# Half of the modulation's weight pieces multiplied in plain f32, and the small first loads issued by ScalarE

## The chip, the cores and the metric

The kernel runs on one core of a Trainium2 chip. The metric is the device time of one execution in microseconds, the lower the better. The engines are named as the profile does: PE is TensorE (PEld its loading of weights), DVE is VectorE, ACT is ScalarE, POOL is GpSimd and SP is SyncE, which issues nearly all DMA transfers here.

## The reference, cut to what matters

The kernel computes one layer of a generator block over 1024 latent tokens and 256 context tokens, each of width 1024. Everything begins with the modulation: a conditioning vector `c` for the latent tokens and `c_ctx` for the context go through SiLU and are multiplied by the same weight `w_ada` of 1024 x 6144.

```
mod  = silu(c)     @ w_ada + b_ada
modc = silu(c_ctx) @ w_ada + b_ada
sh1, sc1, gt1, sh2, sc2, gt2 = split(mod, 6)          # csh1, csc1, ... = split(modc, 6)
h  = rmsnorm(x,   g_mix) * (1 + sc1)  + sh1
hc = rmsnorm(ctx, g_mix) * (1 + csc1) + csh1
p  = h @ w_in                                         # and columns of hc @ w_in
...                                                   # three groups of heads, w_out, residual, mixture of experts
```

The change lies in the first third of `mod` and `modc`: the columns 0 to 2047 of `w_ada`, which give `sh1` and `sc1` for both kinds of token. Nothing of the projection `h @ w_in` can begin before they are there.

## The kernel before, in words

The kernel goes through the modulation and the norm of the tokens (lines 245 to 347), the four projections by 512 columns of `w_in` (lines 349 to 510), the three head groups, and the experts. In the part that is touched the order of the instructions on each engine comes from the tile framework, which orders them by a timeline of its own; the head groups and the experts have an order written by a planner in the kernel and are not touched.

**The modulation.** The 2048 columns are four groups `g` of 512, and each group has eight pieces `k` of 128 rows: 32 pieces of 128x512 f32, 256 KB each. SP loads them (line 239), the first five ahead of everything else (line 250). A piece goes into one of 21 slices of buffers that are needed only later (`bu`, `qc`, `yc`, `vc`, `kc`); the pieces 21 to 31 use the slices of the pieces 0 to 10 a second time.

PE multiplies in a reduced form of f32 (`fp32r`) in the kernel before. To keep the precision a piece is split in two: ACT copies it into `wh`, rounded (line 227), and DVE subtracts, which gives the rest `wl` (line 228). For some pieces of `w_in` POOL does the subtraction.

```
def split_piece(w, slow=False):
    h = wspl.tile([128, 512], F32R, name="wh")
    l = wspl.tile([128, 512], F32R, name="wl")
    nc.scalar.activation(h, w, AF.Copy)
    (nc.gpsimd if slow else nc.vector).tensor_sub(l, w, f32(h))
    return h, l
```

The stationary operand is `csx`, four columns for each `k`: the rounded SiLU of `c` and of `c_ctx`, and the rests of both. Two products for each piece add into `pm`, 4x512 in PSUM (line 299): `csx` with `wh` for all four rows, and the two rounded columns with `wl` for the first two rows.

`csx` comes from six small transfers into `rows`, a tile of 48x128 (lines 252 to 257): `c`, `c_ctx`, a part of `b_ada`, `g_mix`, and `bs_tok` twice. PE transposes `rows` (line 259), DVE copies it to `cols` (261), ACT applies SiLU, which needs a load of its table (263), and DVE makes `csx` (266, 267).

After the eight pieces of a group DVE copies `pm` to `mr` (306), PE transposes it in four steps into `acc` (308), and DVE adds the bias and makes the shift `mcol` and the scale `acol` (311 to 316). The tile `mr` and the tile `hf` below have one common buffer (tag `hf`, one buffer).

**The tokens.** Tiles of 128 tokens are loaded (`load_x`, line 272), the two context tiles first, among the pieces of the last group; ACT and DVE make the norm, PE transposes (330), ACT applies scale and shift into `hf` (334), and DVE splits it as well (345, 346). The first projection product (line 377) needs this for the first half of the first context tile, and the split pieces of `w_in`, whose loads stand on SP behind the pieces of the modulation.

Of the kernel before, what the change touches and what calls it, by code (L numbers as in the profile page):

```python
# [11 lines left out]
F32 = mybir.dt.float32  # L12
# [11 lines left out]
KD = D // 128  # L24
# [130 lines left out]
def f32(ap):  # L155
    return ap.bitcast(F32)
# [7 lines left out]
def block_kernel(ctx: ExitStack, tc: tile.TileContext, A, out):  # L164
    nc = tc.nc
# [47 lines left out]
    with ExitStack() as p1:  # L213
# [10 lines left out]
# [6 lines that stand above are left out]
# [7 lines left out]
        def load_piece(c0, k, src="w_in"):  # L237
            w = early.pop(0) if early else wraw.tile([128, 512], F32, name="wr")
            nc.sync.dma_start(w, A[src][0, k * 128:(k + 1) * 128, c0:c0 + 512])
            return w  # L240
# [4 lines left out]
        with ExitStack() as p0:  # L245
            stage = p0.enter_context(tc.tile_pool(name="stage", bufs=2))
# [2 lines left out]

            ahead = [load_piece(0, k, "w_ada") for k in range(AH)]  # L250
            rows = stage.tile([48, 128], F32, bufs=1)
            nc.sync.dma_start(rows[0:8], A["c"].rearrange("a (k p) -> (a k) p", p=128))
            nc.sync.dma_start(rows[8:16], A["c_ctx"].rearrange("(k p) -> k p", p=128))
            nc.sync.dma_start(rows[16:32], A["b_ada"][0:1, 0:2048].rearrange("a (k p) -> (a k) p", p=128))
            nc.sync.dma_start(rows[32:40], A["g_mix"].rearrange("a (k p) -> (a k) p", p=128))
            nc.sync.dma_start(rows[40:44], A["bs_tok"][0])
            nc.sync.dma_start(rows[44:48], A["bs_tok"][0])
            pr = psT.tile([128, 512], F32, name="pT")
            nc.tensor.transpose(pr[:, :48], rows, ident[:48, :48])
            cols = consts.tile([128, 48], F32)  # L260
# [3 lines left out]
            cs2 = cs.rearrange("p (j k) -> p k j", j=2)  # L264
            csx = stage.tile([128, KD, 4], F32R, bufs=1)
            nc.vector.tensor_copy(csx[:, :, 0:2], cs2)
            nc.vector.tensor_sub(csx[:, :, 2:4], cs2, f32(csx[:, :, 0:2]))

            def load_x(tt):
                x = stage.tile([128, D], F32, name="x")  # L270
                src = A["ctx"][0, tt * 128:(tt + 1) * 128] if tt < 2 else A["x"][0, (tt - 2) * 128:(tt - 1) * 128]
                nc.sync.dma_start(x, src)
                junk = stage.tile([128, D], BF, name="junk", bufs=1)
                st = stage.tile([128, 4], F32, name="st", bufs=3)
                nc.scalar.activation(junk, x, AF.Square, accum_out=st[:, 0:1])
                nc.vector.tensor_scalar(st[:, 1:2], st[:, 0:1], 1.0 / D, EPS, op0=OP.mult, op1=OP.add)
                nc.scalar.activation(st[:, 2:3], st[:, 1:2], AF.Sqrt)
                nc.vector.reciprocal(st[:, 3:4], st[:, 2:3])
                nc.vector.tensor_scalar(x, x, st[:, 3:4], None, op0=OP.mult)
                return x  # L280
# [7 lines left out]
            def take_x(i):  # L288
                if i in XG:
                    xs[len(xs)] = load_x(len(xs))  # L290

            for g in range(4):
                pm = psM.tile([4, 512], F32, name="pm")
                for k in range(KD):
                    take_x(g * KD + k)
                    h, l = split_piece(ahead.pop(0) if ahead else load_piece(g * 512, k, "w_ada"))
                    turns = [(pm, csx[:, k, :], h), (pm[0:2], csx[:, k, 0:2], l)]
                    for i, (o, c, x) in enumerate(turns if k < KD - 1 else turns[::-1]):
                        nc.tensor.matmul(o, lhsT=c, rhs=x, start=(k + i == 0), stop=(k + i == KD))
                if g == 3:  # L300
                    raw_c = []
                    for k in range(KD):
                        take_x(4 * KD + k)
                        raw_c.append((load_piece(1536, k), k % 2 == 1))
                mr = stage.tile([4, 512], F32, name="mr", tag="hf", bufs=1)
                nc.vector.tensor_copy(mr, pm)
                for n in range(4):
                    nc.tensor.transpose(pc[:, g * 16 + n * 4:g * 16 + n * 4 + 4], mr[:, n * 128:(n + 1) * 128], ident[:4, :4])
                chunk = slice(g * 4, g * 4 + 4)
                parts = pc[:, g * 16:g * 16 + 16].rearrange("p (n i j) -> p i j n", i=2, j=2)  # L310
                nc.vector.tensor_tensor(mcol[:, :, chunk], parts[:, 0],
                                        cols[:, None, 16 + g * 4:20 + g * 4].to_broadcast([128, 2, 4]), op=OP.add)
                nc.vector.tensor_add(mcol[:, :, chunk], mcol[:, :, chunk], parts[:, 1])
                if g > 1:
                    kk = slice(g * 4 - 8, g * 4 - 4)
                    nc.vector.scalar_tensor_tensor(acol[:, :, kk], mcol[:, :, chunk], 1.0,
                                                   cols[:, None, 24 + g * 4:28 + g * 4].to_broadcast([128, 2, 4]),
                                                   op0=OP.add, op1=OP.mult)
# [4 lines left out]
            for tt in range(10):  # L323
                x = xs[tt] if tt in xs else load_x(tt)
                j = 1 if tt < 2 else 0
                for half in range(2):
                    pt = psT.tile([128, 512], F32, name="pT")
                    for i in range(4):
                        k = half * 4 + i
                        nc.tensor.transpose(pt[:, i * 128:(i + 1) * 128], x[:, k * 128:(k + 1) * 128], ident)  # L330
                    hf = stage.tile([128, 4, 128], F32, name="hf", tag="hf", bufs=1)
                    for i in range(4):
                        k = half * 4 + i
# [182 lines left out]
    with ExitStack() as p2:  # L516
# [212 lines left out]
        ahead = {}  # L729
# [166 lines left out]
        for u in range(NU):  # L896
            h, t = divmod(u, 8)
# [30 lines left out]
    with ExitStack() as p4:  # L928
# [13 lines left out]
        def tiles(name, width, n, dt=F32, pool=one):  # L942
            return [pool.tile([128, width], dt, name=f"{name}{i}") for i in range(n)]
# [8 lines left out]
            A=tiles("A", 512, 6, pool=psF), T=tiles("T", 512, 2, pool=psF))  # L952
# [78 lines left out]
        for i in range(16):  # L1031
            n, k = divmod(i, KD)
# [309 lines left out]
        k = TILE * NT + 20  # L1342
# [224 lines left out]
        for r in ORDER:  # L1567
# [5 lines left out]
            start = max(t0, tl)  # L1573
# [104 lines left out]
```

## Time and profile before

| | |
|---|---|
| median of three runs | 1212.03 us |
| lowest and highest of them | 1210.14, 1726.21 us |
| the profiled execution, its own time | 1222.53 us |
| its span, first to last instruction | 1220.8 us |
| PE busy / DVE busy / ACT busy / POOL busy | 88% / 76% / 61% / 35% |

The span is that of one execution under the profiler. A busy share is a mean over the span, whose stages have different limits. A line such as "18.35 0.41 PE L308 MATMUL acc<-ident,mr 4*128 4x4 f32 x4 [0.47 <-DVE mr]" says: at 18.35 us the first of four instructions of line 308 began, together they end 0.41 us later, they write `acc` and read `ident` and `mr`, and in brackets, where there are any, how long the engine was idle before and what ended that. PE's products are pipelined, so one can begin while the former still runs: the distance between two starts is the time that one holds the engine. The SP lines are issues of transfers, not their duration.

### The profile page before, as it was taken

To read this page: it belongs to the slowest core of one execution; us is meant where nothing else is said; L and a number is where in the kernel's file an instruction comes from. 1 tells how busy PE (TensorE), PEld (TensorE's weight loads), DVE (VectorE), ACT (ScalarE), POOL (GpSimd) and SP (SyncE) were. 2 spreads that over 40 slices of the span, in tenths; PEclk is the share of its full clock that TensorE was granted. 3 is DMA by queue.
4 is the path that set the end of the run, shared out by engine and by line. 5 is a ranking of instruction groups with operands and counts; after the bars stand their busy time and mean duration, and the time that the engine had idled before them with its cause. 6 is when DMAs were issued, how large, how long until landed. Compare 5 with 4: busy or idle time off the path is not lost. (4 is left out here: it accounts for less than half of the span.)

```text
span 1220.8 us, 18543 instructions
## 1 busy us (share of the span) xinstructions
PE 1071.8 (88%) x5620; PEld 845.5 (69%) x5620; DVE 927.3 (76%) x1758; ACT 743.9 (61%) x1469; POOL 422.2 (35%) x426
## 2 busy tenths in 40 slices
PE   6899989978999999988899888898898898898880
PEld 1688667766888888877687676666666676666650
DVE  7676779657889788886668987776887767678965
ACT  7774123028889898886643543465766666566763
POOL 0200001013798888875424342122233122322220
PEclk9999999989999999998899986999999999899985
DMA  8625664010000000000355636488998978898986
GB/s 316 219 70 167 200 220 132 1 47 1 18 1 19 1 1 27 1 10 1 109 188 163 194 123 220 134 265 251 275 287 260 285 216 246 240 290 278 262 283 246
DMA packets 99980, 191.30 MB, mean 157 GB/s; under 512 B 17720, under 2 KB 19560, under 8 KB 99750
## 3 DMA queue, kind: packets, MB, share of 16 engines
q1 hardware_dynamic: 93606, 172.59, 42.9%
q0 software_dynamic: 6272, 17.51, 6.5%
q8 instruction: 45, 0.74, 0.2%
q14 instruction: 57, 0.47, 0.1%
HBM read 168.95 MB, written 24.07 MB: 158 GB/s over the span
## 5 line engine op out<-in xcount | busy, mean ns | idle before, releaser
L645 DVE TENSOR_REDUCE st<-SC 128x1 f32<-128x1280 f32 x64 | 95.2, 1487 | 35.3 <-PE SC L640 32.8
L377 PE MATMUL acc<-wh,hH 128*128 128x512 f32 x256 | 101.1, 396 | 3.5 <-ACT bu L477 1.8
L1009 ACT ACTIVATE W<-R 128x512 fp32r<-128x512 f32 x118 | 73.3, 628 | 49.0 <-DMA R<-in_w_up_dram 16.6
L378 PE MATMUL acc<-wl,hH 128*128 128x512 f32 x256 | 101.4, 397 | 0.0
L379 PE MATMUL acc<-wh,hL 128*128 128x512 f32 x256 | 100.9, 394 | 0.0
L986 DVE TENSOR_TENSOR W<-R,W 128x512 fp32r<-128x512 f32 x107 | 74.1, 707 | 28.0 <-ACT W L1009 26.8
L1022 PE MATMUL A<-W,XP 128*128 128x512 f32 x223 | 92.8, 416 | 1.9 <-ACT W L1009 1.9
L648 ACT ACTIVATE P<-SC,st 128x1280 f32<-128x1280 f32 x64 | 85.2, 1331 | 11.7 <-DVE st L645 9.9
L1023 PE MATMUL A<-W,XP 128*128 128x512 f32 x223 | 90.6, 406 | 1.9 <-DVE W L986 1.6
L1024 PE MATMUL A<-W,XP 128*128 128x512 f32 x223 | 89.6, 402 | 0.0
L580 ACT ACTIVATE PT<-T 128x512 f32<-128x512 f32 (+1 forms) x126 | 65.5, 549 | 12.1 <-PE T L576 11.2
L692 PE MATMUL T<-vc,PT 128*128 128x64 f32 x512 | 63.4, 278 | 0.0
L640 PE MATMUL SC<-KC,QC 128*128 128x512 f32 (+1 forms) x192 | 53.9, 390 | 9.3 <-ACT P L648 9.3
L692 PEld LDWEIGHTS T<-vc,PT 128*128 128x128 f32 x512 | 61.4, 196 | 0.9 <-ACT PT L580 0.5
L804 DVE TENSOR_REDUCE ast<-SA 128x1 f32<-128x640 f32 (+1 forms) x64 | 50.2, 784 | 13.3 <-PE SA L795 7.9
L377 PEld LDWEIGHTS acc<-wh,hH 128*128 128x128 f32 x256 | 48.4, 189 | 15.0 <-issue 2.9
L379 PEld LDWEIGHTS acc<-wh,hL 128*128 128x128 f32 x256 | 48.4, 189 | 11.5 <-issue 1.0
L378 PEld LDWEIGHTS acc<-wl,hH 128*128 128x128 f32 x256 | 48.4, 189 | 10.4 <-issue 0.7
L402 DVE SCALAR_TENSOR_TENSOR macc<-mw,cs,macc 128x512 f32<-128x512 f32 x56 | 41.8, 747 | 17.8 <-DMA mw<-in_w_ada_dram 17.6
L1022 PEld LDWEIGHTS A<-W,XP 128*128 128x128 f32 x223 | 43.6, 195 | 15.4 <-ACT W L1009 3.2
L1023 PEld LDWEIGHTS A<-W,XP 128*128 128x128 f32 x223 | 43.4, 195 | 14.1 <-DVE W L986 5.0
L576 PE MATMUL T<-ident,P 128*128 128x128 f32 x320 | 47.6, 277 | 2.5 <-DVE P L657 1.6
(715 smaller groups left out, 3235.5 us busy)
## 6 DMA issues: line engine op xcount, KB each, us to landing
R<-in_w_up_dram SPq DMA_DIRECT2D x74, 256.0 KB
R<-in_w_gate_dram SPq DMA_DIRECT2D x73, 256.0 KB
R<-in_w_down_dram SPq DMA_DIRECT2D x73, 256.0 KB
mw<-in_w_ada_dram SPq DMA_DIRECT2D x64, 256.0 KB
wr<-in_w_in_dram SPq DMA_DIRECT2D x32, 256.0 KB
kv<-in_w_gate_dram SPq DMA_DIRECT2D x20, 256.0 KB
late_vcB<-in_w_up_dram SPq DMA_DIRECT2D x19, 256.0 KB
kv<-in_w_down_dram SPq DMA_DIRECT2D x19, 256.0 KB
```

Of the source, the lines that this page charges most:

```text
L377: nc.tensor.matmul(acc[:, n0:n1], lhsT=a, rhs=W[k][0][:, n0:n1], start=(k == 0), stop=False)
L378: nc.tensor.matmul(acc[:, n0:n1], lhsT=a, rhs=W[k][1][:, n0:n1], start=False, stop=False)
L379: nc.tensor.matmul(acc[:, n0:n1], lhsT=b, rhs=W[k][0][:, n0:n1], start=False, stop=(k == KD - 1))
L580: nc.scalar.activation(dst, src, AF.Copy)
L645: nc.vector.tensor_reduce(small[0][:, j:j + 1], buf(("SC", u, j))[:, 0:1280], axis=AX.X, op=OP.max, negate=True)
L648: nc.scalar.activation(buf(("P%d" % j, u)), buf(("SC", u, j))[:, 0:1280], AF.Exp, bias=small[0][:, j:j + 1], accum_out=small[0][:, 2 + j:3 ...
L692: nc.tensor.matmul(buf(O)[:, 0:64], lhsT=buf(("PT", u, g))[:, (c - c0) * 128:(c - c0 + 1) * 128], rhs=vc[c // 8][:, c % 8, h * 64:(h + 1) ...
L986: (nc.gpsimd if engine == "POOL" else nc.vector).tensor_sub(dst, a, b)
L1009: h = add("ACT", 0.5, (key, "sh"), lambda: nc.scalar.activation(buf(value)[:, 0:512], raw(), AF.Copy), r=r, w=[value], after=[chain["split ...
L1022: nc.tensor.matmul(acc, lhsT=ah, rhs=w[:, 0:512], start=first, stop=False)
L1023: nc.tensor.matmul(acc, lhsT=ah, rhs=w[:, 512:1024], start=False, stop=False)
L1024: nc.tensor.matmul(acc, lhsT=al, rhs=w[:, 0:512], start=False, stop=last)
```

## The change

The six small transfers are issued by ACT's queue and not by SP's. A second stationary operand `csf` is made: four columns for each `k` in plain f32, the unrounded SiLU of `c` and `c_ctx`, and two columns of zeros. The pieces with an odd `k` are no longer split: one product in plain f32, `csf` with the piece itself, adds to all four rows of `pm`. The pieces with an even `k` are split and multiplied as before; as the last piece of a group is an odd one, the turned order of its two products falls away.

```diff
             rows = stage.tile([48, 128], F32, bufs=1)
-            nc.sync.dma_start(rows[0:8], A["c"].rearrange("a (k p) -> (a k) p", p=128))
-            nc.sync.dma_start(rows[8:16], A["c_ctx"].rearrange("(k p) -> k p", p=128))
...
+            nc.scalar.dma_start(rows[0:8], A["c"].rearrange("a (k p) -> (a k) p", p=128))
+            nc.scalar.dma_start(rows[8:16], A["c_ctx"].rearrange("(k p) -> k p", p=128))
...
             nc.vector.tensor_sub(csx[:, :, 2:4], cs2, f32(csx[:, :, 0:2]))
+            csf = stage.tile([128, KD, 4], F32, bufs=1)
+            nc.gpsimd.memset(csf, 0.0)
+            nc.vector.tensor_copy(csf[:, :, 0:2], cs2)
...
                 for k in range(KD):
                     take_x(g * KD + k)
-                    h, l = split_piece(ahead.pop(0) if ahead else load_piece(g * 512, k, "w_ada"))
-                    turns = [(pm, csx[:, k, :], h), (pm[0:2], csx[:, k, 0:2], l)]
-                    for i, (o, c, x) in enumerate(turns if k < KD - 1 else turns[::-1]):
-                        nc.tensor.matmul(o, lhsT=c, rhs=x, start=(k + i == 0), stop=(k + i == KD))
+                    piece = ahead.pop(0) if ahead else load_piece(g * 512, k, "w_ada")
+                    if k % 2:
+                        nc.tensor.matmul(pm, lhsT=csf[:, k, :], rhs=piece, start=False, stop=(k == KD - 1))
+                        continue
+                    h, l = split_piece(piece)
+                    nc.tensor.matmul(pm, lhsT=csx[:, k, :], rhs=h, start=(k == 0), stop=False)
+                    nc.tensor.matmul(pm[0:2], lhsT=csx[:, k, 0:2], rhs=l, start=False, stop=False)
```

The other four of the six transfers are moved in the same way.

## Rows read from the trace of the kernel before

**Rows 1.** The page, its first part: busy time of PE and PEld, their share of the span and their instructions.

```profile
PE 1071.8 (88%) x5620; PEld 845.5 (69%) x5620; DVE 927.3 (76%) x1758; ACT 743.9 (61%) x1469; POOL 422.2 (35%) x426
```

**Rows 2.** Busy time of each engine in a long stretch behind the modulation. The columns are the length of the stretch, the busy time (and instructions) of PE, PEld, DVE, ACT and POOL, the granted clock, the busy share of the DMA engines, and GB/s.

```profile
40.00:140.00 100.00, 98.73 (x484) 81.64 (x484) 65.61 (x145) 52.34 (x137) 3.80 (x4) 0.99 0.44 141
```

**Rows 3.** PE's products in order of time: the transpose of `rows`, the first and some later products into `pm`, the first round of L308 and the product behind it, the last product, the last round of L308, the start of the projection, and the eight transposes of one tile of tokens.

```profile
8.80 0.31 PE L259 MATMUL pT<-ident,rows 48*128 48x48 f32 x1 [8.80 <-DMA rows<-in_bs_tok_dram]
10.17 0.58 PE L299 MATMUL pm<-wh,csx 128*4 128x512 f32 x1 [1.06 <-DVE csx L267]
...
14.82 0.59 PE L299 MATMUL pm<-wl,csx 128*2 128x512 f32 x1
15.25 0.39 PE L299 MATMUL pm<-wh,csx 128*4 128x512 f32 x1
15.48 0.40 PE L299 MATMUL pm<-wl,csx 128*2 128x512 f32 x1
...
18.35 0.41 PE L308 MATMUL acc<-ident,mr 4*128 4x4 f32 x4
18.69 0.39 PE L299 MATMUL pm<-wl,csx 128*2 128x512 f32 x1
...
35.00 0.39 PE L299 MATMUL pm<-wh,csx 128*4 128x512 f32 x1
37.07 0.41 PE L308 MATMUL acc<-ident,mr 4*128 4x4 f32 x4 [1.68 <-DVE mr L306]
...
39.83 0.78 PE L377 MATMUL acc<-wh,hctx 128*128 128x512 f32 x1
...
56.27 1.04 PE L330 MATMUL pT<-ident,x 128*128 128x128 f32 x8
```

**Rows 4.** ACT in order of time at the end of the modulation: the last three pieces, and the first `hf`.

```profile
31.50 1.67 ACT L227 ACTIVATE wh<-yc 128x512 fp32r<-128x512 f32 x3 [0.16 <-issue]
...
37.52 1.51 ACT L334 ACTIVATE hf<-pT,mcol,acol 128x128 f32<-128x128 f32 x4 [1.28 <-PE acc L308]
```

**Rows 5.** DVE in order of time at the same place: a subtraction for `w_in`, and the copy of the last `mr`.

```profile
34.64 1.77 DVE L228 TENSOR_TENSOR wl<-wr,wh 128x512 fp32r<-128x512 f32 x1
36.34 0.67 DVE L306 COPY mr<-pm 4x512 f32<-4x512 f32 x1
```

**Rows 6.** The stretches of one microsecond, with the columns of rows 2.

```profile
6.00:7.00 1.00, 0.00 (x0) 0.00 (x0) 0.20 (x1) 0.84 (x2) 0.00 (x0) 1.00 0.26 92
7.00:8.00 1.00, 0.00 (x0) 0.00 (x0) 1.00 (x2) 1.00 (x2) 0.00 (x0) 1.00 0.18 44
...
16.00:17.00 1.00, 1.00 (x6) 0.37 (x5) 1.00 (x2) 0.97 (x2) 0.00 (x0) 1.00 1.05 404
...
31.00:32.00 1.00, 1.00 (x5) 0.65 (x4) 0.85 (x4) 0.84 (x3) 0.00 (x0) 0.50 1.05 385
```

**Rows 7.** A stretch of ten microseconds, with the same columns.

```profile
20.00:30.00 10.00, 7.86 (x33) 2.06 (x31) 8.69 (x21) 8.96 (x15) 0.00 (x0) 0.94 1.05 393
```

**Rows 8.** The groups of instructions by line between 0 and 130 us, one line for each shape: the two steps of a split for the pieces in `bu`. The columns are the busy time, the mean length of one in ns, and the idle time before.

```profile
L228 DVE TENSOR_TENSOR wl<-bu,wh 128x512 fp32r<-128x512 f32 x8 | 5.2, 685 | 3.7 <-ACT wh L227 3.7
L227 ACT ACTIVATE wh<-bu 128x512 fp32r<-128x512 f32 x8 | 5.0, 628 | 3.0 <-DMA bu<-in_w_ada_dram 2.9
```

**Rows 9.** PE in order of time around a product in plain f32 of another stage (L449, two records), with a product in the reduced form before and behind it.

```profile
229.17 0.40 PE L378 MATMUL acc<-wl,hH 128*128 128x512 f32 x1
229.40 1.02 PE L449 MATMUL pr<-yc,wsT 128*128 128x512 f32 x2
229.86 0.80 PE L379 MATMUL acc<-wh,hL 128*128 128x512 f32 x1
```

**Rows 10.** The issues on SP in order of time: the first pieces, the first, the fifth and the sixth of the small loads, the next pieces, the first pieces that use a slice a second time, and the last pieces.

```profile
0.76 1.82 SPq L239 DMA_DIRECT2D bu<-in_w_ada_dram  x4
...
3.10 0.38 SPq L252 DMA_DIRECT2D rows<-in_c_dram  x1
...
4.56 0.29 SPq L256 DMA_DIRECT2D rows<-in_bs_tok_dram  x1
6.13 0.25 SPq L257 DMA_DIRECT2D rows<-in_bs_tok_dram  x1
6.79 1.45 SPq L239 DMA_DIRECT2D qc<-in_w_ada_dram  x3
...
16.63 1.67 SPq L239 DMA_DIRECT2D bu<-in_w_ada_dram  x3
...
23.36 2.30 SPq L239 DMA_DIRECT2D yc<-in_w_ada_dram  x3
```

**Rows 11.** ACT in order of time at the start: the table load, the first splits, and the table load for SiLU.

```profile
0.75 1.28 ACT L227 ACT_TABLE_LOAD   x1 [0.75 <-PEq L1666]
3.90 1.24 ACT L227 ACTIVATE wh<-bu 128x512 fp32r<-128x512 f32 x2 [1.87 <-DMA bu<-in_w_ada_dram]
6.13 1.29 ACT L227 ACTIVATE wh<-bu 128x512 fp32r<-128x512 f32 x2 [0.99 <-DMA bu<-in_w_ada_dram]
...
8.07 1.28 ACT L263 ACT_TABLE_LOAD   x1
```

**Rows 12.** POOL in order of time: its first instruction after the constants of the start.

```profile
34.34 3.20 POOL L228 TENSOR_TENSOR wl<-wr,wh 128x512 fp32r<-128x512 f32 x2 [32.77 <-ACT wh L227]
```

More of the change, by code (lines that the diff above doesn't have):

```diff
@@ L251, in block_kernel @@
             rows = stage.tile([48, 128], F32, bufs=1)
-            nc.sync.dma_start(rows[0:8], A["c"].rearrange("a (k p) -> (a k) p", p=128))
-            nc.sync.dma_start(rows[8:16], A["c_ctx"].rearrange("(k p) -> k p", p=128))
[L254 to L257, printed above, removed]
+            nc.scalar.dma_start(rows[0:8], A["c"].rearrange("a (k p) -> (a k) p", p=128))
+            nc.scalar.dma_start(rows[8:16], A["c_ctx"].rearrange("(k p) -> k p", p=128))
+            nc.scalar.dma_start(rows[16:32], A["b_ada"][0:1, 0:2048].rearrange("a (k p) -> (a k) p", p=128))
+            nc.scalar.dma_start(rows[32:40], A["g_mix"].rearrange("a (k p) -> (a k) p", p=128))
+            nc.scalar.dma_start(rows[40:44], A["bs_tok"][0])
+            nc.scalar.dma_start(rows[44:48], A["bs_tok"][0])
             pr = psT.tile([128, 512], F32, name="pT")
```

## The prediction

> **What bounds the kernel now.** I read the page first, then the stretches of ten microseconds, then each engine's instructions in order of time. The page says that PE is busy for 88% of the span [rows 1]. That is a mean over many stages, so the stage of the change has to be looked at alone. It is the first 40 us: the modulation. From 40 us on PE has hardly a gap (98.7 of the next 100 us busy, [rows 2]), so whatever moves the first projection (L377, at 39.83, [rows 3]) moves everything behind it by as much (the later stages start from its data), and what does not move it is worth nothing.
>
> Back from L377: it needs `hctx`, which needs `hf` on ACT (L334, 37.52, [rows 4]). `hf` shares its one buffer with `mr`, so it waits for the four transposes of the last `mr` (L308, 37.07). These wait for the copy of `mr` (DVE, 36.34, [rows 5]). The last product into `pm` had ended at 35.39 (35.00 and 0.39, [rows 3]); the copy came 0.95 later, since DVE was in a 1.77 us subtraction for the next weights [rows 5]. So the end of the products and the state of DVE at that moment set the start of the projection, and 39.83 - 36.34 = 3.49 us of fixed steps follow the copy.
>
> Before that end three things run side by side. The stream of transfers moves about 400 GB/s in its best stretch (404 at 16 us, [rows 6]). DVE is busy 8.69 and ACT 8.96 of 10 us between 20 and 30, PE only 7.86 [rows 7]. So PE waits for the splits, and the splits and the stream are level: the last pieces are split by ACT from 31.50 on [rows 4]. PE is not the bound there; it even fell back to its lower clock level (0.50 at 31 us, 1.2 GHz, [rows 6]) after a stretch with gaps.
>
> **The change, part by part. What the odd pieces lose.** Sixteen of the 32 pieces lose one ACT copy (0.628 us) and one DVE subtraction (0.685 us, [rows 8]): 10.0 us of ACT and 11.0 us of DVE, out of a stretch of about 30 us. This takes both off the bound. On PE they lose two products, 0.23 apart at the upper clock level [rows 3], 0.455 a pair.
>
> **What they gain.** One product in plain f32 with 4 columns of weight. The trace has no such shape. The nearest row is L449, 128 columns of weight and the same 512 columns streamed, two records to a product [rows 9]. L378 before it ends at 229.17 + 0.40 = 229.57, L379 behind it at 229.86 + 0.80 = 230.66; take L379's own 0.23 away and the f32 product held PE for 0.86 us. Ends: 0.455, if few columns made it as cheap as the pair that it replaces, and 1.02, the length of the two records together. I take 0.86, as the same number of columns is streamed. PE's work for a pair of pieces goes from 0.91 to 1.32 us, and 16 pairs take 21.1 us where they took 14.6. The stream gives a pair in about 1.3 us (2 x 262 KB at 404 GB/s), so PE now runs level with the stream and cannot catch up after a late start.
>
> **The small transfers.** On SP the six loads of `rows` stand behind five pieces and ahead of the sixth. They start at 3.10, one every 0.365 us up to the fifth at 4.56; the sixth leaves only at 6.13, in the moment in which ACT is released by the landing of the third piece [rows 10, 11], and the next piece leaves at 6.79. I read this as eight transfers in flight at most: the eleventh waits for the third. The transfers of 3.69 us are missing from the stream: 92 and 44 GB/s between 6 and 8 us [rows 6]. Taken off SP, this hole closes, and the last piece can be there up to 3.69 us earlier. The trace of before has no DMA issued by ACT. Its cost on ACT lies between nothing, as ACT waits from 2.03 to 3.90 for the first piece anyway [rows 11], and six issues of SP's length, 2.2 us, with or without a wait for the limit of eight; behind them on ACT stand its table load (1.28), the first splits and `cs`, and PE waits for `cs`.
>
> What the stream gains can be held against the Trainium skill, DMA: Bandwidth & Descriptors, section "Issuing engines are not separate DMA queues": transfers from all queues share the same 16 DMA engines, and a second queue only saves the issue time. By that rule the stream would gain an estimated 2.2 us (six issues) and not 3.69; the trace of before, where the hole is longer than the issues, speaks for more, and no run so far shows it.
>
> **When PE can start** is the pivot. From the issue of the last `rows` load to its transpose pass 2.67 us (6.13 to 8.80); from the table load for Silu to the first product 2.10 us (8.07 to 10.17) [rows 3, 10, 11]. If ACT issues all six from 0.75 on without a wait, they are out at 2.9 and landed at 5.3; the first table load ends at 4.2, two splits at 5.5, and the products start at 5.5 + 2.1 = 7.6. If the last issues wait for the first piece (3.90), the same steps give 4.2, 5.5, 6.75 and 8.85. If they wait for the third piece as now (6.13), 11.0. I take the middle of the first two, 8.2, because on two queues the small loads no longer all stand behind five large ones.
>
> **The sum.** From its first product PE needs 21.1 us for the pieces, 1.0 for three rounds of L308 (0.34 each, 18.35 to 18.69), 1.0 for the eight transposes of a context tile (L330, 56.27), and 2.5 for the lower clock at the start: from 10.17 to 15.25 products are 0.43 apart, then 0.23, so half of 5.08 us is lost [rows 3]. That is 25.6 us, and 8.2 + 25.6 = 33.8. The copy of `mr` finds DVE free and starts at 33.9, not 36.34: **2.4 us earlier**. The stream (28.9 at best) and ACT and DVE are done before that.
>
> Edits that I cost at nothing: the memset of `csf` (POOL is idle until 34 us, [rows 12]), its copy on DVE (0.2 us beside the first split; if it stood ahead of `csx`, PE would start 0.2 later). A new wait: pieces 21 to 31 are loaded into the buffers of 0 to 10, and the odd ones are now freed by PE, not by DVE. Before, the first of these loads leaves at 16.63 [rows 10]; PE would be done with piece 1 at about 10.8 and with piece 9 at about 18, while the load that reuses it is the second of the last three, near 24.2 before, and now leaves at 20.5 at the earliest. So SP, with the context tiles and `w_in` queued behind, does not stall; if PE were over 2.5 us later it would.
>
> The profiled execution took 1222.53 us, 1220.8 of them span, 10.5 more than the median of the runs, 1212.03. I carry the difference over as it is: 1220.1 for a profiled execution, **1209.6** for the median.
>
> **The rivals.** *The stream sets the end.* If PE starts early or the f32 product costs less than 0.86, the last piece decides: its split starts by 32.6 now (the third of those from 31.50), so it would land at 28.9; with 0.86 for its product and 0.1 the copy starts at 29.9, 6.4 us earlier: 1205.6. For it: half of the ACT and DVE work is gone. Against it: PE's 25.6 us from any start after 5 us end later. By the rule of the Trainium skill named above (an estimate) this case gives 5.0 us and 1207.0.
>
> *PE becomes the bound and is late* (the slower side). It decides where the products start after 36.34 - 0.1 - 25.6 = 10.6. With the old wait for the third piece (11.0) the copy starts at 36.7, 0.4 later than before; with 1.02 for the f32 product 2.5 more: 1214.9. For it: ACT works in order, so a waiting issue holds up splits and `cs`. Against it: the `rows` loads can start 2.3 us earlier than on SP.
>
> *The gain is given back before L377.* ACT and DVE reach the splits of `w_in` sooner, and these, with POOL's, can stand ahead of `mr` or `hf` again as the 1.77 us did. A 2.4 us gain is two such instructions: 1212.0.
>
> **How the numbers follow.** Forecast 0.45 (1207.5 to 1211.5), stream 0.2, late PE 0.2, given back 0.15. The range goes from the stream's 1205.6, less 2 for a clock that no longer falls around 30 us, to the late PE's 1214.9 and 1 for the spread of the runs: 1203.5 to 1216. A chance of 2% (24 us) either way is small, since the whole stage is 40 us: 0.02 faster, 0.96 within, 0.02 slower. 2% is about what a measurement of this kernel can tell from no change.
>
> **What would show it.** First product into `pm` near 8.2; an f32 product every 1.32 us and PE without gaps from there to about 33.8; DVE and ACT with gaps between 10 and 30; no hole in the stream at 6 to 8 us; the copy of `mr` right behind the last product; L377 at about 37.4. I am wrong if PE shows gaps before the end of the products, if ACT sits on a DMA issue until 6 us, or if the later stages are ordered anew and move by more than the first one.

## The result and the profile after

The changed kernel takes 1224.64 us (median of 20 runs, 1214.14 to 1238.95), the kernel before in the same comparison 1214.62 (median of 20). The ratio is 1.0064, with an interval from 1.0037 to 1.0092: slower by 4.5 to 11.2 us. The medians are over all runs, the ratio over the fast ones alone, without the few that ran over 1.5% above the fastest. I had forecast 2.4 us less than before and a range that ended at 1216.0, so the sign and the range were both wrong. The execution that was profiled took 1238.95 us, more than all others of its kernel; its first 60 us, on which the reading rests, agree within 0.6 us with a second profile of the same kernel (a_again below). Lines 268 to 295 of before stand three higher (the load of a token tile, L272, is now L275), those behind 305 six: L377 is now L383, L306 is L312, L330 is L336, L334 is L340; the products into `pm` are L304 (`wh`), L305 (`wl`) and L301 (plain f32).

The first part of the page, to be held against [rows 1]:

```profile
PE 1085.1 (88%) x5620; PEld 851.5 (69%) x5620; DVE 918.0 (74%) x1743; ACT 733.8 (59%) x1453; POOL 424.0 (34%) x427
```

DVE and ACT lost 9.3 and 10.1 us, about what the change takes off them, and nothing came of it. Where the time went is seen on ACT in order of time, from its first issue on (ACTq is the issue of a transfer; compare [rows 10, 11]):

```profile
0.76 0.59 ACTq L252 DMA_DIRECT2D rows<-in_c_dram  x1
...
2.08 0.33 ACTq L255 DMA_DIRECT2D rows<-in_g_mix_dram  x1
3.63 0.26 ACTq L256 DMA_DIRECT2D rows<-in_bs_tok_dram  x1
4.03 0.26 ACTq L257 DMA_DIRECT2D rows<-in_bs_tok_dram  x1
4.31 1.28 ACT L227 ACT_TABLE_LOAD   x1 [4.31 <-DMA rows<-in_bs_tok_dram]
5.61 1.25 ACT L227 ACTIVATE wh<-bu 128x512 fp32r<-128x512 f32 x2
7.51 0.63 ACT L227 ACTIVATE wh<-qc 128x512 fp32r<-128x512 f32 x1 [0.65 <-DMA qc<-in_w_ada_dram]
9.30 0.63 ACT L227 ACTIVATE wh<-qc 128x512 fp32r<-128x512 f32 x1 [1.16 <-DMA qc<-in_w_ada_dram]
9.95 1.28 ACT L263 ACT_TABLE_LOAD   x1
11.24 0.22 ACT L263 ACTIVATE cs<-cols 128x16 f32<-128x16 f32 x1
```

The fifth issue waits 1.2 us, until the first piece has landed (3.61 in the trace's semaphore events). Then four splits stand ahead of the table load for SiLU, and the third and fourth of them wait for their pieces. `cols` had been there since 8.78; `cs` is made at 11.24. PE shows the same from the other side ([rows 3] for before), with the last products, the first projection and, between them, the transposes of a token tile:

```profile
8.22 0.31 PE L259 MATMUL pT<-ident,rows 48*128 48x48 f32 x1 [8.22 <-DMA rows<-in_bs_tok_dram]
12.02 0.59 PE L304 MATMUL pm<-wh,csx 128*4 128x512 f32 x1 [3.49 <-DVE csx L267]
...
17.39 0.39 PE L304 MATMUL pm<-wh,csx 128*4 128x512 f32 x1
17.62 0.40 PE L305 MATMUL pm<-wl,csx 128*2 128x512 f32 x1
17.95 1.02 PE L301 MATMUL pm<-qc,csf 128*4 128x512 f32 x2
18.90 0.40 PE L304 MATMUL pm<-wh,csx 128*4 128x512 f32 x1
...
34.99 0.60 PE L336 MATMUL pT<-ident,x 128*128 128x128 f32 x4
35.75 1.02 PE L301 MATMUL pm<-qc,csf 128*4 128x512 f32 x2
36.70 0.66 PE L336 MATMUL pT<-ident,x 128*128 128x128 f32 x4
...
39.60 1.02 PE L301 MATMUL pm<-yc,csf 128*4 128x512 f32 x2
41.39 0.41 PE L314 MATMUL acc<-ident,mr 4*128 4x4 f32 x4 [0.77 <-DVE mr L312]
45.59 1.11 PE L336 MATMUL pT<-ident,x 128*128 128x128 f32 x4 [3.80 <-ACT hf L340]
46.36 0.78 PE L383 MATMUL acc<-wh,hctx 128*128 128x512 f32 x1
```

The first projection starts at 46.36, 6.53 us later than before. Four terms make this up. The products start 1.85 later (12.02 for 10.17). They take 28.60 us (12.02 to 40.62) where they took 25.22: 3.38. A pair of pieces costs 1.51 us (17.39 to 18.90), and with `wh` and `wl` taken at 0.455 of it as before, a plain product costs PE 1.055 us. The copy of `mr` follows the last product after 0.04 and not 0.95 (against [rows 5]): -0.91.

```profile
40.66 0.68 DVE L312 COPY mr<-pm 4x512 f32<-4x512 f32 x1 [0.27 <-PE pm L301]
```

The last term, 2.21, lies between `mr` and the first projection, which are now 5.70 apart and were 3.49. There ACT stands still:

```profile
41.47 1.06 ACT L278 ACTIVATE junk<-x 128x1024 bf16<-128x1024 f32 x1 [6.90 <-DMA x<-in_x_dram]
...
43.51 0.63 ACT L227 ACTIVATE wh<-wr 128x512 fp32r<-128x512 f32 x1 [0.90 <-DMA wr<-in_w_in_dram]
44.05 1.49 ACT L340 ACTIVATE hf<-pT,mcol,acol 128x128 f32<-128x128 f32 x4
```

The square of the third token tile and a piece of `w_in` now stand ahead of the first `hf` in ACT's order. Both wait for transfers, and SP shows why these are late:

```profile
25.23 3.64 SPq L239 DMA_DIRECT2D wr<-in_w_in_dram  x5
37.39 0.33 SPq L275 DMA_DIRECT2D x<-in_x_dram  x1
37.81 3.56 SPq L239 DMA_DIRECT2D wr<-in_w_in_dram  x5
```

SP issues nothing from 28.87 to 37.39. The third tile needs a slot of the two token buffers, and the slot comes free with the transposes that now stand at 34.99 and 36.70 among the late products. The rest of `w_in` is queued behind. In the kernel before, all eight stood together and earlier, and the load followed them:

```profile
29.90 1.91 PE L330 MATMUL pT<-ident,x 128*128 128x128 f32 x8
```

```profile
31.84 0.33 SPq L272 DMA_DIRECT2D x<-in_x_dram  x1
```

The stretches, with the columns of [rows 6], show the empty stream, and that the hole at 6 to 8 us is mostly filled and the clock at 31 us is at its upper level:

```profile
6.00:7.00 1.00, 0.00 (x0) 0.00 (x0) 0.73 (x2) 0.86 (x2) 0.00 (x0) 1.00 0.76 285
7.00:8.00 1.00, 0.00 (x0) 0.00 (x0) 0.58 (x1) 0.49 (x1) 0.00 (x0) 1.00 0.66 165
31.00:32.00 1.00, 1.00 (x4) 0.18 (x4) 0.67 (x2) 1.00 (x3) 0.00 (x0) 1.00 1.05 387
33.00:38.00 5.00, 5.00 (x23) 1.81 (x23) 4.14 (x6) 1.56 (x3) 3.58 (x3) 1.00 0.03 7
```

A little more is lost right behind the first projection. The granted clock is 0.50 there from 44.5 to 51.3 us, after PE had waited 3.80 us for `hf`; before, it was 0.50 from 39.2 to 42.5. The first product with `hH`, the rounded latent tokens, stands at 61.10 for 53.54, which is 7.56 later.

### The profile page after: what moved, and what is told of

Same layout as the page of the kernel before. It is cut to its first block, busy times and chain, and to the rows that moved or that the text cites. A ratio compares the mean times of both kernels' runs of the same rounds, so it can differ in the third digit from the quotient of the medians.

```text
span 1237.2 us, 18485 instructions
## 1 busy us (share of the span) xinstructions
PE 1085.1 (88%) x5620; PEld 851.5 (69%) x5620; DVE 918.0 (74%) x1743; ACT 733.8 (59%) x1453; POOL 424.0 (34%) x427
## 5 line engine op out<-in xcount | busy, mean ns | idle before, releaser
L651 DVE TENSOR_REDUCE st<-SC 128x1 f32<-128x1280 f32 x64 | 95.2, 1487 | 37.4 <-PE SC L646 35.1
L383 PE MATMUL acc<-wh,hH 128*128 128x512 f32 x256 | 101.0, 396 | 1.7 <-ACT bu L483 1.0
L1015 ACT ACTIVATE W<-R 128x512 fp32r<-128x512 f32 x118 | 73.1, 627 | 44.5 <-DMA R<-in_w_up_dram 14.5
L1028 PE MATMUL A<-W,XP 128*128 128x512 f32 x223 | 95.0, 426 | 2.5 <-ACT W L1015 2.5
L1029 PE MATMUL A<-W,XP 128*128 128x512 f32 x223 | 92.2, 413 | 1.5 <-DVE W L992 1.4
L1030 PE MATMUL A<-W,XP 128*128 128x512 f32 x223 | 91.9, 412 | 0.0
L383 PEld LDWEIGHTS acc<-wh,hH 128*128 128x128 f32 x256 | 48.1, 188 | 13.6 <-issue 2.4
L1028 PEld LDWEIGHTS A<-W,XP 128*128 128x128 f32 x223 | 44.8, 201 | 15.3 <-ACT W L1015 3.8
L1029 PEld LDWEIGHTS A<-W,XP 128*128 128x128 f32 x223 | 44.6, 200 | 12.3 <-DVE W L992 3.6
L1030 PEld LDWEIGHTS A<-W,XP 128*128 128x128 f32 x223 | 44.5, 199 | 10.1
```

Of the source, the lines that this page charges most:

```text
L383: nc.tensor.matmul(acc[:, n0:n1], lhsT=a, rhs=W[k][0][:, n0:n1], start=(k == 0), stop=False)
L651: nc.vector.tensor_reduce(small[0][:, j:j + 1], buf(("SC", u, j))[:, 0:1280], axis=AX.X, op=OP.max, negate=True)
L1015: h = add("ACT", 0.5, (key, "sh"), lambda: nc.scalar.activation(buf(value)[:, 0:512], raw(), AF.Copy), r=r, w=[value], after=[chain["split ...
L1028: nc.tensor.matmul(acc, lhsT=ah, rhs=w[:, 0:512], start=first, stop=False)
L1029: nc.tensor.matmul(acc, lhsT=ah, rhs=w[:, 512:1024], start=False, stop=False)
L1030: nc.tensor.matmul(acc, lhsT=al, rhs=w[:, 0:512], start=False, stop=last)
```

## The experiments

### Each part alone: e1_queue_only and e2_plain_only

e1_queue_only is the kernel before with the six small transfers on ACT's queue, e2_plain_only the changed kernel with them back on SP's. The edit for e1 is the same line six times,

```diff
-            nc.sync.dma_start(rows[0:8], A["c"].rearrange("a (k p) -> (a k) p", p=128))
+            nc.scalar.dma_start(rows[0:8], A["c"].rearrange("a (k p) -> (a k) p", p=128))
```

and the reverse for e2.

> The kernel before with the six small loads issued by ACT, all pieces still split. Theory A (the changed kernel's loss of 6.5 us at the first projection product is made of a start 1.85 us later, products that hold PE 3.4 us longer, and 2.2 us of waiting for a weight piece of w_in): the queue alone moves the first product into pm to 10 to 12 us, closes the hole in the stream at 6 to 8 us, and the first projection product starts between 38.5 and 41 (before 39.83): ratio 0.999 to 1.002. Theory B (the issues on ACT are the whole loss): first projection product at 44 or later, ratio 1.004 or more.

> The changed kernel with the six small loads back on SP. Theory A: first product into pm near 10.2 as before, then 28.6 us of products, so the last copy of mr at 38.9 and the first projection product between 42.4 and 44.6 (the second if the wait for w_in stays): ratio 1.002 to 1.005. Theory B: without the issues on ACT the plain products are a gain, first projection product before 39.8, ratio below 1.000.

Measured: e1 1215.47 us, ratio 1.0021 (0.9989 to 1.0053); e2 1219.45, ratio 1.0049 (1.0024 to 1.0073). The first product and the first projection, of e1 and then of e2:

```profile
13.41 0.58 PE L299 MATMUL pm<-wh,csx 128*4 128x512 f32 x1 [5.43 <-DVE csx L267]
...
41.35 0.78 PE L377 MATMUL acc<-wh,hctx 128*128 128x512 f32 x1
```

```profile
9.90 0.58 PE L304 MATMUL pm<-wh,csx 128*4 128x512 f32 x1 [1.29 <-DVE csx L267]
...
42.42 0.78 PE L383 MATMUL acc<-wh,hctx 128*128 128x512 f32 x1
```

The queue alone makes the products start 3.24 us later than before, at 13.41 and not at the 10 to 12 that I had expected (seven splits stand ahead of SiLU's table load on ACT, and two subtractions ahead of the last step of `csx` on DVE). Still the products end at 34.04, 1.35 earlier: there PE is not the bound, and they take 20.6 us for 25.2. The gain is given back on DVE, where two long steps for what comes later stand ahead of `mr`, and the projection is 1.52 late, 0.35 beyond the range of theory A:

```profile
33.82 1.69 DVE L279 TENSOR_SCALAR x<-x,st 128x1024 f32<-128x1024 f32 x1
35.43 1.75 DVE L228 TENSOR_TENSOR wl<-wr,wh 128x512 fp32r<-128x512 f32 x1
37.11 0.67 DVE L306 COPY mr<-pm 4x512 f32<-4x512 f32 x1
```

With the plain products alone PE starts in time and ends late: `mr` is copied at 39.12, and the projection and the ratio lie where theory A had them. Neither shows the stall in front of `hf`; in e2 that square stands at 42.72, behind the first `hf`.

### Why a plain product costs 1.055 us: e3_wide

The weight of the plain products is padded with zeros to 128 columns, and `pm` to 128 rows; so that all rows are opened, the first product of a group uses a padded weight as well. To fit, there are eight buffers for split pieces and not nine.

```diff
-            csf = stage.tile([128, KD, 4], F32, bufs=1)
+            csf = stage.tile([128, KD, 128], F32, bufs=1)
...
-                pm = psM.tile([4, 512], F32, name="pm")
+                pm = psM.tile([128, 512], F32, name="pm")
```

> The changed kernel with the plain f32 weight padded with zeros to 128 columns (and one splitting buffer less of nine, to make room). Theory A1 (the narrow weight is what makes a plain product cost 1.06 us where the row of 128 columns gave 0.86): distance between two pairs of pieces falls from 1.51 to 1.32 us, the products take 25.5 us from first to last, the first projection product is near 43.3. Theory A2 (the change from one form of f32 to the other costs 0.1 us each time, whatever the width): 1.51 us stays.

One run, 1222.78 us, too little to judge the time by, but its steps can be read. In order of time, in e3_wide (L304 is the plain product here, L307 `wh`, L308 `wl`):

```profile
20.17 0.39 PE L308 MATMUL pm<-wl,csx 128*2 128x512 f32 x1
20.40 1.02 PE L304 MATMUL pm<-yc,csf 128*128 128x512 f32 x2
20.86 0.80 PE L307 MATMUL pm<-wh,csx 128*4 128x512 f32 x1
21.49 0.39 PE L308 MATMUL pm<-wl,csx 128*2 128x512 f32 x1
```

A pair takes 1.32 us (20.17 to 21.49), the figure of the prediction, and the plain product 0.865: thirty-two times as many columns of weight are 0.19 us cheaper. `mr` is copied at 38.61 and the first projection starts at 43.28, 3.08 earlier than in the changed kernel (4.67 lie between the two, so 1.18 of the stall is still there). The weight loads of both, the changed kernel first:

```profile
17.95 0.09 PEld L301 LDWEIGHTS pm<-qc,csf 128*4 128x4 f32 x2 [0.47 <-issue]
18.90 0.08 PEld L304 LDWEIGHTS pm<-wh,csx 128*4 128x4 f32 x1 [0.86 <-issue]
```

```profile
20.18 0.42 PEld L304 LDWEIGHTS pm<-yc,csf 128*128 128x128 f32 x2
```

The four columns are loaded when their product begins (17.95, both), and the next load begins with the next product too (18.90); the 128 columns are loaded from 20.18 on, 0.22 ahead of their product at 20.40, while the one before still runs. That the width decides (of the weight, and with it of the rows of `pm`) is shown, and f2_early_wide below has the same 1.32; that the cost is the load which is not hidden is what these records say, without a test of its own.

### The stall for the tokens: e4_three_x

The changed kernel with a third token buffer, and eight buffers for split pieces to make room:

```diff
-                x = stage.tile([128, D], F32, name="x")
+                x = stage.tile([128, D], F32, name="x", bufs=3)
```

> The changed kernel with three buffers for the token tiles (and one splitting buffer less of nine). Theory A: SP no longer waits for a token buffer between 29 and 37 us with the rest of w_in queued behind it; the transfers run on through 33 to 38 us, the first hf follows the last mr at once, and the first projection product starts near 44.1 instead of 46.4: ratio to before 1.003 to 1.006. Rival (hf is late for another reason, the order on ACT or the tokens): 46.4 stays.

Measured: 1222.15 us, ratio 1.0071 (1.0038 to 1.0104). SP, ACT, DVE and PE of e4_three_x:

```profile
29.57 6.79 SPq L275 DMA_DIRECT2D x<-in_x_dram  x2
```

```profile
35.58 1.06 ACT L278 ACTIVATE junk<-x 128x1024 bf16<-128x1024 f32 x1 [0.60 <-DMA x<-in_x_dram]
...
40.56 1.50 ACT L340 ACTIVATE hf<-pT,mcol,acol 128x128 f32<-128x128 f32 x4 [3.83 <-PE acc L314]
```

```profile
39.39 0.67 DVE L312 COPY mr<-pm 4x512 f32<-4x512 f32 x1
```

```profile
42.88 0.78 PE L383 MATMUL acc<-wh,hctx 128*128 128x512 f32 x1
```

The third tile leaves from 29.57 on, its square is done before `hf` is due, and `hf` follows the last `mr` at once: 42.88 - 39.39 = 3.49 from the copy to the projection, the fixed steps of before. So the buffer was the cause of the 2.21 (and not the eight buffers for split pieces, as e3 has eight too and keeps 1.18 of the stall). The other 1.27 by which this projection is earlier than in the changed kernel are not the buffer's: in this execution the products at the start stand at the wider distance until 14.53 and not until 17.39, and `mr` is copied 1.27 earlier. The time doesn't show the gain: the ratio lies above the 1.003 to 1.006 that I expected, and an interval of 8 us is too wide for a gain of 2.

### An early start: the four f kernels

All four issue the small transfers on SP ahead of the pieces and load the SiLU table at once, with one activation of a single column. f1_early has the narrow plain products, f2_early_wide the padded ones, f3_early_quarter plain products for every fourth piece only (the last line below), and f4_early_split none.

```diff
+            warm = stage.tile([128, 1], F32, bufs=1)
+            nc.scalar.activation(warm, ident[:, 0:1], AF.Silu)
+            nc.sync.dma_start(rows[0:8], A["c"].rearrange("a (k p) -> (a k) p", p=128))
...
             ahead = [load_piece(0, k, "w_ada") for k in range(AH)]
...
-                    if k % 2:
+                    if k % 4 == 3:
```

> The changed kernel with the six small loads on SP ahead of all pieces, and a SiLU of one column at the start, so that ACT loads that table before anything else. Nothing else is changed: half of the pieces are still multiplied in plain f32. Theory A (late start, longer products, then SP waiting for a token buffer add up): the first product into pm falls from 12.0 to about 7, the products still take 28.6 us and end at 35.6, the first projection product is at 39.2 (41.4 if the wait for w_in stays): ratio 0.999 to 1.002. Rival (the order of the work behind the first product sets the end, not its start): the first projection product stays at 42 or later.

> The same early start with the plain f32 weight padded to 128 columns (one splitting buffer less). Theory A: 1.32 us for two pieces, products from 7 to 32.5 us, now level with the stream; the first projection product near 36 (38.3 if the wait for w_in stays), 1.5 to 4 us before the kernel before: ratio 0.996 to 0.999. Rival: the stream or the splits of w_in hold it at 39 or later, ratio 1.000 or more.

> The same early start, and only every fourth piece in plain f32 with the narrow weight. Theory A: PE has 20 us of products and is no longer the bound; the stream is, the last piece lands near 31 and the first projection product starts between 35.5 and 38: ratio 0.996 to 0.999. Rival (DVE and ACT bound it again with 24 splits): 39 or later.

> The kernel before with the small loads ahead of all pieces on SP and the table for SiLU loaded at the start, all pieces split. Theory A: first product near 7, but DVE and ACT have 32 splits each (21 to 22 us) and the last copy of mr still waits for DVE: first projection product between 37 and 40, ratio 0.997 to 1.001. Rival (the start was all that mattered in the kernel before): 36.5 or earlier.

| | first product | copy of the last `mr` | first projection | median us | ratio |
|---|---|---|---|---|---|
| f1_early | 6.56 | 35.37 | 38.57 | 1218.61 | 1.0062 (1.0033 to 1.0090) |
| f2_early_wide | 6.67 | 34.07 | 37.58 | 1213.27 | 0.9998 (0.9965 to 1.0030) |
| f3_early_quarter | 6.67 | 34.99 | 38.19 | 1215.31 | 1.0007 (0.9978 to 1.0036) |
| f4_early_split | 6.55 | 35.97 | 39.47 | 1215.37 | 1.0012 (0.9978 to 1.0046) |

The SiLU of f1_early, on ACT, is done at 4.87 where the changed kernel ends it at 11.46:

```profile
0.75 1.28 ACT L252 ACT_TABLE_LOAD   x1 [0.75 <-PEq L1674]
...
4.65 0.22 ACT L265 ACTIVATE cs<-cols 128x16 f32<-128x16 f32 x1 [2.41 <-DVE cols L263]
```

With all pieces split a start 3.6 us earlier than before brings the projection 0.36 us forward (f4): PE waits for the splits and the start is not its limit. With plain products it is: f1 starts 5.46 earlier than the changed kernel, its copy of `mr` 5.29 and its projection 7.79, as the stall is gone too. The projections of f2 and f3 came within the wider bounds that I had set or 0.2 behind them, but neither ratio shows the gain that I expected, 0.996 to 0.999. And f1 was slower than before although its projection is 1.26 earlier. That didn't fit.

### The first stage by itself: s_before, s_after, s_f1, s_f2, s_e1, s_e2

The kernel can end behind the projections (its constant STOP). Attention, router and experts are left out, and the four to six runs of such a kernel lie within 2.3 to 5.3 us of each other, those of the whole kernel before within 21 (1204.71 to 1225.99).

```diff
-STOP = None
+STOP = 1
```

> The kernel before, ended behind the first stage (the modulation, the projections and the gate): attention, router and experts are left out. It is the base for the three kernels beside it, which are to be compared with it and not with the whole kernel. From the trace of before, whose projections end at about 290 us, both theories expect 290 to 310 us.

> The changed kernel, ended at the same place (attention, router and experts are left out). Theory A, the projections start late and what follows moves with them: 6.5 us over s_before, the 6.53 us by which the first projection starts later in the trace of after, or less where the gate takes some of it back. Theory B, the whole loss of 10 us arises in this stage: 10 us over s_before. Theory C, the stage takes its late start back and the loss arises behind it: 2 us or less over s_before.

> f1_early ended at the same place (attention, router and experts are left out): the small rows ahead of the weights on the first queue, the Silu table loaded early, 16 plain products with four weight columns. Its first projection started at 38.57 us (before 39.83). Theory A: 1.3 us under s_before, or the same; then the 0.6% by which the whole kernel was slower lies behind the stage. Theory B: 4 to 5 us over s_before.

> f2_early_wide ended at the same place (attention, router and experts are left out): as s_f1, with the plain products' weight padded to 128 columns. Its first projection started at 37.58 us (before 39.83). Theory A: 2.2 us under s_before, or the same, and 1 us under s_f1. Theory B, which has the narrow products' cost in this stage: 1 us under s_before, and 5 to 6 us under s_f1.

> e1_queue_only (the kernel before with the six rows on ScalarE's queue, nothing else) ended behind the first stage; attention, router and experts are left out. Its first projection stood at 41.35 us, 1.5 us behind before's. If the end of the stage follows the first projection: 264.9 us, 1.5 over s_before's 263.3. If the queue alone costs what the start of the first product showed in the whole change (1.85 us) and the stall behind it too: 267 us.

> e2_plain_only (the changed kernel with the six rows back on SyncE's queue) ended behind the first stage; attention, router and experts are left out. Its first projection stood at 42.42 us, 2.6 us behind before's. If the end of the stage follows the first projection: 265.9 us, and the two parts add up to 4.1 us of the 6.8 of both together, the rest being the stall for the tokens that arises only where both come together. If the plain products hold more than that: 268 us or more.

| ended behind the first stage | median us | against s_before | first projection against before |
|---|---|---|---|
| s_before | 263.33 (262.14 to 266.18) | | |
| s_after | 270.09 (268.40 to 271.16) | +6.76 | +6.53 |
| s_e1 (queue alone) | 264.29 (262.70 to 267.99) | +0.96 | +1.52 |
| s_e2 (plain products alone) | 265.60 (263.83 to 267.19) | +2.27 | +2.59 |
| s_f1 | 263.68 (261.64 to 265.10) | +0.35 | -1.26 |
| s_f2 | 262.28 (261.26 to 263.53) | -1.05 | -2.25 |

The last column is from the whole kernels. I had expected 290 to 310 us for the base, which was too long; the differences are what counts. Each carries an estimated 1.5 to 2 us either way, from the scatter of the runs; without the one run of s_before that stands apart, 266.18, all would be 0.2 higher. The late end, 6.76 us, is well clear of that and agrees with the 6.53, so it arises in the first 46 us in the main and is not taken back.

The parts alone make 0.96 + 2.27 = 3.23 of it, but only roughly: s_e1 and s_e2 ran on another chip than the other four, and the whole kernel before took 1217.73 us there and 1212.35 on theirs. By the first projections they make 1.52 + 2.59 = 4.11 of the 6.53, and the other 2.42 arise only where both come together. That is nearly the stall of 2.21, which needs products so late that the transposes are spread among them. That a late start also counts in full where PE has no spare time is argued from the traces alone (12.02 against 9.90 in e2 is 2.12, and a later start cost less in e1).

Whether an early projection comes out at the end of the stage is not shown. The medians of s_f1 and s_f2 stand 0.35 above and 1.05 below s_before, within the scatter; in the profiled executions the last product of the projections stands at 256.42 and 256.01 against 257.90. One execution is no sure measure either: the first projection of these stopped kernels stands at 40.23 (s_before), 45.36 (s_after), 39.26 (s_f1) and 36.80 (s_f2), up to one microsecond from that of the whole kernels.

### Once more: a_again, f1_again, f2_again, and a plain delay: g_delay

Three kernels unaltered, and f2_early_wide with five passes of GpSimd over the zeros of the padded weight between the SiLU and the weights (`csx` is then made from `csf`, so that it waits too):

```diff
             nc.gpsimd.memset(csf, 0.0)
+            for _ in range(5):
+                nc.gpsimd.tensor_scalar(csf, csf, cs[:, 0:1], None, op0=OP.mult)
             nc.vector.tensor_copy(csf[:, :, 0:2], cs2)
```

> The changed kernel once more, unaltered, for its loss beside the others of this call. If the loss is the late end of the first stage and nothing else, 6.8 us (s_after against s_before) over the kernel before: ratio 1.0056. If there is a loss behind the stage as well, 10 us: 1.008.

> f1_early once more, unaltered. If the loss arises in the first stage alone, the 0.35 us of s_f1 against s_before, ratio 1.000, and the 1.0062 measured the first time was no property of the kernel. If sixteen narrow plain products cost something behind the stage, 1.004 to 1.006 again.

> f2_early_wide once more, unaltered. If the first stage alone decides, 1.05 us under the kernel before (s_f2 against s_before), ratio 0.999; it is the fastest of the kernels tried in this stage, and by the other theory it stands 5 to 6 us under f1_again.

> f2_early_wide with nothing but a delay ahead of the first product: five passes of GpSimd over the padded weight's zeros stand between the Silu and the weights, estimated at 5 to 8 us from the 0.94 us of the memset and the 1.66 us of the subtraction on that engine. If a late end of the first stage passes whole into the end of the kernel, the time rises over f2_again by what the first projection is later in the trace (37.58 us in f2_early_wide). If later stages take a delay back, by less than half of it.

| | median us | ratio |
|---|---|---|
| a_again | 1225.79 | 1.0082 (1.0052 to 1.0111) |
| f1_again | 1217.25 | 1.0001 (0.9964 to 1.0037) |
| f2_again | 1215.06 | 1.0000 (0.9970 to 1.0030) |
| g_delay | 1238.78 | 1.0172 (1.0132 to 1.0212) |

f1's loss of 0.6% did not come back. As its first stage ends 0.35 us from that of before, I take it for no property of the kernel, though its two intervals barely meet and a loss of up to 4 us is not excluded. The changed kernel's loss did come back. Its two intervals, 4.5 to 11.2 and 6.3 to 13.5 us, both hold the 6.76 of the first stage. The second ratio, 1.0082, stands at the value that I expected for a loss behind the stage as well, but doesn't exclude the other; whether some microseconds more are lost there stays open. The passes of g_delay, by line:

```profile
L270 POOL TENSOR_SCALAR csf<-csf,cs 128x1024 f32<-128x1024 f32 x5 | 14.2, 2846 | 3.1 <-ACT cs L265 2.7
```

One pass took 2.85 us and not the 1 to 1.6 that I had estimated, and behind the passes, which end at 19.81, the steps that make the weights stood behind steps for a token tile in DVE's order until 26.30. So the delay became 19.9 us and not 5 to 8 at the first product (26.45 for 6.59 in f2_again) and 20.6 at the first projection (57.87 for 37.24). The whole kernel rose by 23.7 us between the medians (its six runs: 1230.62 to 1241.37): within that scatter a delay ahead of the first projection comes out at the end whole.

## Why the prediction was wrong

**The bound** was read rightly: the first projection sets the stage, and a delay of it passes through (g_delay, s_after). That a gain passes through as well, as I wrote, is not shown: s_f2 stands 1.05 under s_before, within the scatter, and the interval of the whole f2 (0.9965 to 1.0030) holds a gain of its 2.25 us as well as none.

**When PE can start: 8.2 forecast, 12.02 measured.** This is the pivot that failed. The case with a wait for the first piece came true (the fifth issue at 3.63, the last out at 4.29), for which the steps gave 8.85. They counted two splits ahead of SiLU's table load; the order of ACT has four, and the last two wait for their pieces, until 9.93. From the table load to the first product it is then 2.07 us, as reckoned (2.10). The landing was mis-sized too: `rows` is transposed 4.19 us after its last issue, not 2.67; `cols` at 8.78 would be the limit next, if the table were loaded early. The point from which the late rival decides, 10.6, was passed. So it is this rival, with its chance of 0.2, that came true in kind; it priced the loss at 2.9 us, and 4.5 to 11.2 were measured.

**The plain product: 0.86 forecast, 1.055 measured**, outside my bounds (0.455 to 1.02), since L449 [rows 9] has 128 columns and I reasoned that only the columns streamed count. Sixteen times 0.195 is 3.1 us, all of the 3.0 by which the products (28.6) exceed the sum's 25.6. With a weight of 128 columns (e3) the step holds to 0.01. The sum's 2.5 for a slow start was near: the products stand at the wider distance from 12.02 to 17.39. That this is the clock, as I wrote, rests on the distances alone; the view's granted clock reads 1.00 from 12.00 to 17.40, and before from 10 to 15.

**The slot reuse.** I wrote that SP stalls if PE is over 2.5 us later, and looked at the pieces alone. PE was late, and the stall came through the token buffers: 2.21 us, taken away by e4.

**What held.** DVE and ACT came off the bound, the hole at 6 to 8 us was mostly filled, the copy of `mr` follows the last product, and the clock, 0.50 at 31 us before [rows 6], was at its upper level there, with no gaps on PE. The eight transfers in flight, as I read from SP, are there in the semaphore events of the changed kernel's trace too: counted over both queues, each transfer from the ninth on waits for the landing of the one eight places ahead. ACT's fifth, at 3.63, waits for the first piece (3.61), its sixth, at 4.03, for `c_ctx` (4.01), and SP's sixth piece, at 4.45, for the second (4.44). The events show eight semaphores used in turn, so this is how the program hands them out. On the rule of the Trainium skill, DMA: Bandwidth & Descriptors, section "Issuing engines are not separate DMA queues" (another queue saves issue time alone): the first piece into a used slice left at 15.25, 1.38 earlier than before [rows 10], less than the 2.2 us of issue time and far from my 3.69. That agrees with the rule, though these loads may have waited for buffers.

Put together: 12.02 for 8.2 is 3.8 us, 28.6 for 25.6 is 3.0, and the stall 2.2. Together they make the 9.0 us between the projection forecast, 37.4, and the one measured, 46.36.

## What to carry to other kernels

Before work is moved from the engines that bound a stage to one with spare time, sum that engine's work from its real start: without spare time each late microsecond counts, and where it could catch up (e1) it does not. A small transfer moved to a compute engine's queue is to be judged by what stands in that engine's order between its issue and its consumer; ahead of the large transfers on the old queue, with the table loaded early, it served better. And when a stage shifts by some microseconds, look at every buffer whose release shifts with it, not at those of the changed step alone.

## What the runs showed of the hardware that was not expected

A product in plain f32 with 512 columns streamed cost PE 1.055 us with a weight of four columns and 0.865 us with one of 128: padding with zeros made it faster. The load of the four columns began with the product (17.95), not ahead of it.

For transfers of a few KB, what was in flight counted, and not the queue alone. By the trace's semaphore events the six landed 1.3 to 1.5 us after their issue on SP ahead of all pieces (f1_early), 1.8 to 4.1 us after it on ACT's queue with pieces beside them, and 2.4 to 4.5 us after it behind five pieces on SP (the kernel before).

A multiplication by a column on GpSimd, 128x1024 f32 in place, took 2.85 us.
